# Layer norms of a two-layer encoder: epsilon added on VectorE, and the last token block's statistics taken piece by piece

## The chip, the cores and the metric

The kernel runs on one core of a Trainium2 chip. A core has a matrix engine (TensorE, PE in the rows, with its weight loads as PEld), three engines that work on elements (VectorE as DVE, ScalarE as ACT, GpSimd as POOL), a queue engine that issues most transfers (SyncE, SP), and 16 DMA engines. The metric is the device time of one execution in microseconds, as a median over runs.

## The reference

The reference is an encoder of two layers over 512 tokens of width 1024. Each layer has four phases: a feed-forward half step, a token mixer, an attention into 256 memory tokens, and another feed-forward half step. After each phase stands a post layer norm, so there are eight, each over the 1024 columns of every token:

```python
def layer_norm(x, g, b):
    xf = x.astype(jnp.float32)
    mu = xf.mean(-1, keepdims=True)
    var = jnp.square(xf - mu).mean(-1, keepdims=True)
    return ((xf - mu) * lax.rsqrt(var + LN_EPS) * g.astype(jnp.float32) + b.astype(jnp.float32)).astype(x.dtype)

# each layer:
#   x <- LN(alpha*x + 0.5*SwiGLU_1(x))
#   x <- LN(alpha*x + Mixer_i(x))
#   x <- LN(alpha*x + MemCrossAttn(x, mem))
#   x <- LN(alpha*x + 0.5*SwiGLU_2(x))
```

Everything is in fp32. The mixer of the first layer is a dense attention beside a windowed one, that of the second a neighbourhood attention.

## The kernel before

The eight phases run in the order ffn(0), mixer_ab, memory(0), ffn(1), ffn(2), mixer_c, memory(1), ffn(3). The tokens lie in four blocks of 128, the tiles x_4_85, x_5_86, x_6_87 and x_7_88 (blocks 0 to 3), each 128 x 1024 and resident in SBUF. "The last block" is block 3, x_7_88.

To keep fp32 accuracy, each factor of a product is split into a rounded high part and a rest, and a product is three matmuls (`mm3`: high by high, high by rest, rest by high). The features of x, transposed, lie in xh and xl, one slice of columns per block. Weights are loaded as fp32 (tiles slab and raw), and split by ScalarE (a cast) and VectorE (a subtraction, the TENSOR_TENSOR rows slab<-raw,slab). So VectorE feeds TensorE with weight parts all along, as well as doing its share of the layer norms.

A phase ends in `down` (L538): for each block and each half of 512 columns, six to twelve matmuls into a PSUM bank of tag d or a (each 12 in the mixers and the memory phases, 6 in an FFN, where earlier products have been added to x before), and then one VectorE operation that adds the product to x, x<-d,x or x<-a,x, which also sums what it writes (a DVE_READ_ACCUMULATOR row fetches the sum, into st). There follows `layer_norm` (L505) for the block:

1. nmu<-st, VectorE, one column: minus the mean.
2. slab<-x,nmu,slab, VectorE, 1024 columns: y = (x - mean) * g.
3. junk<-x,nmu, ScalarE: the squares of x - mean, with their sum in var.
4. lny<-var on GpSimd (TENSOR_SCALAR): var / 1024 + epsilon; then lny<-lny,nhalf on GpSimd (TENSOR_TENSOR): that to the power -1/2. Both stand in `rsqrt` (L466).
5. x<-slab,lny,slab, VectorE: y * lny + b. One operation of 1024 columns for blocks 0 and 1, two of 512 for blocks 2 and 3.

After it, in the last phase, each piece goes out by DMA. In the other seven phases `to_features` (L475) makes two rounds of four TensorE transposes (t<-ident,x, 128 x 128 each), one for each half, ScalarE copies each into xh (a cast), and VectorE subtracts for xl (xl<-t,xh). The next phase's products read xh and xl, those of block 3 last of all.

What sets the order: nothing is issued where it stands in the code. All calls are recorded in a graph, and a list scheduler (`plan`, L182, called twice from `emit`, L300) simulates the engines with a table of costs (`cost`, L113) and puts each engine's instructions in an order, which is then fixed; each engine works it off in order, waiting where it has to. The first plan gives each instruction a due time, which is counted back from the order on TensorE; the second plan takes the ready instruction with the earliest due time. Every instruction therefore has line 157 in the profile, and the names of tiles tell what it is. The cost table takes the columns of an instruction from what it writes, except for a reduction:

```python
for d in (out if method != "tensor_reduce" else ins[0]).ap[1:]:
    n *= d[1]
...
if engine == "vector":
    if method == "tensor_scalar" and not wide:
        n = n / 2
    return n / 0.96 + 72 + aside + 60 * scalars + 120 * (method == "scalar_tensor_tensor" and "accum_out" in kw)
```

In ffn the last down product is called from `finish` (L927), for blocks 0 and 1, and then 2 and 3; in the last phase block 2 and block 3 apart.

## Time and profile before

| quantity | value |
|---|---|
| runs, us | 2128.41, 2127.75, 2125.88; median 2127.75 |
| span of the profiled execution | 2123.9 us (no other time of that execution is given) |
| PE busy | 2109.2 us (99%), 12648 matmuls |
| VectorE busy | 1735.8 us (82%), 2500 instructions |
| ScalarE busy | 1161.2 us (55%), 1903 instructions |
| GpSimd busy | 287.4 us (14%), 379 instructions |
| granted TensorE clock | 1.00 for nearly the whole span |
| start of the last matmuls, end of the span | 2111.61 us, 2123.9 us |

Times in rows are microseconds from the span's start. A row of the timeline has start and duration, engine, operation, what is written <- what is read, and how many in a run (x2); a bracket behind it is the engine's idle time before it, and what ended that. Neighbouring operations of a pipelined engine overlap: a row of 0.69 us is often followed 0.61 us after its start. The span lies 3.85 us below the median of the runs.

### The profile page before, as it was taken

How to read it: one execution, taken by the hardware profiler on the slowest of the kernel's cores; microseconds unless marked ns; L12 is line 12 of the kernel's file. 1: busy time of each engine (PE TensorE's matmuls, PEld its weight loads, DVE VectorE, ACT ScalarE, POOL GpSimd, SP SyncE). 2: the span in 40 equal slices, each digit the busy share in tenths (PEclk: the TensorE clock that was granted, in tenths of full speed). 3: DMA queues.
4: the chain of work that ended last, by engine and by line, in shares of the span. 5: the costliest groups of instructions: out<-in, count | busy, mean ns of one | idle time of the engine just before them, and what ended most of it. 6: DMA issues, size and time to landing. Idle time of an engine off the chain costs nothing.

```text
span 2123.9 us, 32745 instructions
## 1 busy us (share of the span) xinstructions
PE 2109.2 (99%) x12648; PEld 1871.0 (88%) x12648; DVE 1735.8 (82%) x2500; ACT 1161.2 (55%) x1903; POOL 287.4 (14%) x379
## 2 busy tenths in 40 slices
PE   9999999999999999999999999999999999999997
PEld 7999988888888899998889999888888888999996
DVE  7789988888748879998879999866577479699997
ACT  5555443698546554545545455457764465444552
POOL 0001015310102000000200000312210021000003
PEclk9999999999999999999999999999999999999999
DMA  6566562004434346564445556356454433456551
GB/s 205 141 168 144 136 191 91 21 18 116 140 125 109 90 117 181 150 158 129 148 100 143 126 139 186 78 147 165 119 165 155 139 93 96 110 149 155 143 149 60
DMA packets 208860, 275.93 MB, mean 130 GB/s; under 512 B 10688, under 2 KB 151616, under 8 KB 208704
## 3 DMA queue, kind: packets, MB, share of 16 engines
q1 hardware_dynamic: 175904, 221.14, 34.0%
q0 software_dynamic: 32512, 52.44, 14.1%
q8 instruction: 100, 1.64, 0.3%
q14 instruction: 56, 0.46, 0.1%
q10 hardware_dynamic: 288, 0.26, 0.0%
HBM read 259.12 MB, written 4.19 MB: 124 GB/s over the span
## 4 chain that ended last, share of the span: by engine, by line
PE 96%; DVE 1%; ACT 1%; DMA 1%; issue 0%; SPq 0%; DVEq 0%; ACTq 0%
PE a L157 59%; PE d L157 23%; PE t L157 15%; DVE slab L157 1%; ACT t L157 1%; DMA slab<-t 1%; DVE x L157 0%; ACT slab L157 0%; SPq L157 0%; DVE t L157 0%; DMA raw<-x_t 0%; ACT xh L157 0%; DVE mn L157 0%; DVE xl L157 0%; DVEq L1662 0%
## 5 line engine op out<-in xcount | busy, mean ns | idle before, releaser
L157 DVE TENSOR_TENSOR slab<-slab,slab 128x1024 fp32r<-128x1024 f32 (+3 forms) x638 | 727.5, 1166 | 69.5 <-ACT slab L157 39.9
L157 ACT CAST slab<-slab 128x1024 fp32r<-128x1024 f32 (+2 forms) x498 | 472.7, 983 | 341.5 <-DVE slab L157 173.2
L157 PE MATMUL a<-slab,slab 128*128 128x256 f32 (+3 forms) x2320 | 567.2, 322 | 0.7 <-DMA slab<-t 0.4
L157 PE MATMUL a<-xh,slab 128*128 128x256 f32 (+2 forms) x2480 | 559.9, 315 | 0.3 <-ACT slab L157 0.3
L157 PE MATMUL d<-slab,slab 128*128 128x512 f32 (+2 forms) x1856 | 447.0, 381 | 0.0
L157 PEld LDWEIGHTS a<-xh,slab 128*128 128x128 f32 x2480 | 416.4, 190 | 33.7 <-ACT slab L157 1.0
L157 PEld LDWEIGHTS a<-slab,slab 128*128 128x128 f32 x2320 | 409.5, 190 | 38.8 <-ACT t L157 1.3
L157 PE MATMUL a<-xl,slab 128*128 128x256 f32 (+1 forms) x1240 | 389.7, 314 | 0.0
L157 PE MATMUL a<-raw,slab 128*128 128x256 f32 x2048 | 388.9, 283 | 0.1
L157 PEld LDWEIGHTS d<-slab,slab 128*128 128x128 f32 x1856 | 329.0, 189 | 55.9 <-issue 0.2
L157 PEld LDWEIGHTS a<-raw,slab 128*128 128x128 f32 x2048 | 327.9, 192 | 5.4 <-ACT slab L157 0.5
L157 PEld LDWEIGHTS a<-xl,slab 128*128 128x128 f32 x1240 | 236.0, 190 | 18.4 <-DVE xl L157 0.4
L157 PE MATMUL t<-slab,slab 128*128 128x512 f32 (+1 forms) x840 | 209.5, 389 | 0.0
L157 DVE TENSOR_TENSOR slab<-raw,slab 128x1024 fp32r<-128x1024 f32 (+2 forms) x140 | 160.2, 1160 | 18.6 <-ACT slab L157 18.4
L157 PEld LDWEIGHTS t<-slab,slab 128*128 128x128 f32 x840 | 149.9, 189 | 26.3
L157 DVE TENSOR_TENSOR slab<-t,slab 128x512 fp32r<-128x512 f32 (+2 forms) x223 | 137.6, 638 | 16.4 <-ACT slab L157 15.9
L157 ACT CAST slab<-t 128x512 fp32r<-128x512 f32 (+2 forms) x223 | 120.9, 566 | 40.7 <-DVE t L157 13.9
L157 ACT CAST slab<-raw 128x1024 fp32r<-128x1024 f32 (+1 forms) x132 | 124.3, 971 | 27.9 <-PE a L157 8.8
L157 DVE SCALAR_TENSOR_TENSOR x<-d,x 128x512 f32<-128x512 f32 x168 | 114.7, 685 | 25.3 <-PE d L157 24.4
L157 ACT COPY t<-a 128x512 f32<-128x512 f32 (+1 forms) x116 | 63.5, 550 | 130.4 <-PE a L157 77.2
L157 POOL DMA_DIRECT2D slab<-ffn_w_down x40 | 47.7, 1193 | 310.3 <-DVE slab L157 276.3
L157 ACT ACTIVATE t<-a 128x512 f32<-128x512 f32 (+3 forms) x65 | 36.3, 559 | 89.0 <-PE a L157 89.0
(126 smaller groups left out, 2167.2 us busy)
## 6 DMA issues: line engine op xcount, KB each, us to landing
slab<-ffn_w_gate SPq DMA_DIRECT2D x80, 512.0 KB
slab<-ffn_w_up SPq DMA_DIRECT2D x80, 512.0 KB
slab<-ffn_w_down SPq DMA_DIRECT2D x80, 512.0 KB
slab<-ffn_w_down POOLq DMA_DIRECT2D x40, 512.0 KB, 5.8
raw<-mem_w_kv SPq DMA_DIRECT2D x16, 1024.0 KB
slab<-t SPq DMA_DIRECT2D x96, 128.0 KB
slab<-ffn_w_gate POOLq DMA_DIRECT2D x16, 512.0 KB, 7.8
slab<-ffn_w_up POOLq DMA_DIRECT2D x16, 512.0 KB, 6.0
```

The source lines that it names most:

```text
L157: op.call = lambda: fn(*args, **kw)
```

## The change

Three things are changed.

- In all eight layer norms, for every block, the step var / 1024 + epsilon moves from GpSimd to VectorE. The power stays on GpSimd.
- For block 3, in all eight, the statistics come from batch-statistics instructions: after each piece of x is added, BN_STATS on VectorE reads that piece and writes six values; after the last, BN_AGGR makes mean and variance of the 18 values (mv). There is then no ScalarE square, no nmu and no accumulated sum for this block, and y = (x - mean) * g is made in two halves.
- For block 3, the second half of the down product, 512 columns in one bank of tag a, becomes two products of 256 columns, one in a bank of tag a and one in a bank of tag d, each with its own addition to x.

```diff
@@ layer_norm
-        nmu = self.small(1, "nmu", 4)
-        nc.vector.tensor_scalar(nmu, st[:, 0:1], st[:, 1:2], -1.0 / D, ALU.add, ALU.mult)
-        var = self.small(1, "var", 4)
...
         y = gb[2][t % 2]
-        nc.vector.scalar_tensor_tensor(out=y, in0=x, scalar=nmu, in1=g, op0=ALU.add, op1=ALU.mult)
-        nc.scalar.activation(self.junk, x, AF.Square, bias=nmu, scale=1.0, accum_out=var)
-        r = self.rsqrt(var, 1, "ln", 1.0 / D, LN_EPS / ALPHA**2)
+        r = self.small(1, "lny", 4)
+        halves = [(0, 512), (512, D)] if t > 1 else [(0, D)]
+        if t == NT - 1:
+            mv = self.small(2, "mv", 2)
+            nc.vector.bn_aggr(out=mv, in_=st)
+            nc.vector.tensor_scalar(r, mv[:, 1:2], LN_EPS / ALPHA**2, None, ALU.add)
+            nc.gpsimd.tensor_tensor(out=r, in0=r, in1=self.nhalf[:, :1], op=ALU.pow)
+            for lo, hi in halves:
+                nc.vector.scalar_tensor_tensor(
+                    out=y[:, lo:hi], in0=x[:, lo:hi], scalar=mv[:, 0:1], in1=g[:, lo:hi], op0=ALU.subtract, op1=ALU.mult
+                )
+        else:
+            nmu = self.small(1, "nmu", 4)
+            nc.vector.tensor_scalar(nmu, st[:, 0:1], st[:, 1:2], -1.0 / D, ALU.add, ALU.mult)
+            var = self.small(1, "var", 4)
+            nc.vector.scalar_tensor_tensor(out=y, in0=x, scalar=nmu, in1=g, op0=ALU.add, op1=ALU.mult)
+            nc.scalar.activation(self.junk, x, AF.Square, bias=nmu, scale=1.0, accum_out=var)
+            nc.vector.tensor_scalar(r, var, 1.0 / D, LN_EPS / ALPHA**2, ALU.mult, ALU.add)
+            nc.gpsimd.tensor_tensor(out=r, in0=r, in1=self.nhalf[:, :1], op=ALU.pow)
         for lo, hi in halves:
             nc.vector.scalar_tensor_tensor(
                 out=x[:, lo:hi], in0=y[:, lo:hi], scalar=r, in1=b[:, lo:hi], op0=ALU.mult, op1=ALU.add
@@ down
         for t in blocks:
-            st = self.small(2, "st", 4) if ln else None
-            for h in range(2):
-                ps = self.ps("da"[h])
+            apart = ln and t == NT - 1
+            st = self.small(18, "bn", 2) if apart else self.small(2, "st", 4) if ln else None
+            cuts = [(0, 512, "d"), (512, 768, "a"), (768, D, "d")] if apart else [(0, 512, "d"), (512, D, "a")]
+            for j, (lo, hi, tag) in enumerate(cuts):
+                ps = self.ps(tag)[:, : hi - lo]
                 for i in range(n):
                     a = [z[:, t * P : (t + 1) * P] for z in acts[i]]
-                    w = [z[:, h * 512 : (h + 1) * 512] for z in wts[i]]
-                    self.mm3(ps, a, w, i == 0, i == n - 1)
-                v = self.x[t][:, h * 512 : (h + 1) * 512]
-                acc = {"accum_out": st[:, h : h + 1]} if ln else {}
+                    self.mm3(ps, a, [z[:, lo:hi] for z in wts[i]], i == 0, i == n - 1)
+                v = self.x[t][:, lo:hi]
+                acc = {"accum_out": st[:, j : j + 1]} if ln and not apart else {}
                 nc.vector.scalar_tensor_tensor(out=v, in0=ps, scalar=coef, in1=v, op0=ALU.mult, op1=ALU.add, **acc)
+                if apart:
+                    nc.vector.bn_stats(out=st[:, 6 * j : 6 * j + 6], in_=v)
```

The cost table prices BN_STATS by the six values it writes, 6 / 0.96 + 72, about 78 ns in the planner, whatever it reads. The scheduler's order changes with the instructions. Three places follow, each as the order of one engine. In the names, x_6_87 and x_7_88 are blocks 2 and 3, d_ and a_ PSUM banks, t_ the banks of transposes, st, nmu, var, lny, bn and mv the small tiles, xh_83 and xl_84 the features, and slab the rest (weights, g, b and y).

First, VectorE in the last phase, from the last addition to x of block 2 to its end. Before:

```order
L157 TENSOR_SCALAR nmu_3848<-st_3845 128x1
L157 SCALAR_TENSOR_TENSOR x_7_88<-d_3851,x_7_88 128x512
L157 SCALAR_TENSOR_TENSOR x_4_85<-slab_3832,lny_3833,slab_3826 128x1024
L157 SCALAR_TENSOR_TENSOR x_5_86<-slab_3839,lny_3840,slab_3826 128x1024
L157 SCALAR_TENSOR_TENSOR x_7_88<-d_3851,x_7_88 128x512
L157 SCALAR_TENSOR_TENSOR x_7_88,st_3852<-d_3853,x_7_88 128x512
L157 SCALAR_TENSOR_TENSOR x_7_88,st_3852<-a_3854,x_7_88 128x512
L157 TENSOR_SCALAR nmu_3855<-st_3852 128x1
L157 SCALAR_TENSOR_TENSOR slab_3832<-x_6_87,nmu_3848,slab_3825 128x1024
L157 SCALAR_TENSOR_TENSOR slab_3839<-x_7_88,nmu_3855,slab_3825 128x1024
L157 SCALAR_TENSOR_TENSOR x_6_87<-slab_3832,lny_3850,slab_3826 128x512 x2
L157 SCALAR_TENSOR_TENSOR x_7_88<-slab_3839,lny_3857,slab_3826 128x512 x2
```

And with the change (the rows just before these are x_5_86 normed, one addition to x_7_88, x_4_85 normed and nmu_3849 for block 2):

```order
L157 SCALAR_TENSOR_TENSOR x_7_88<-d_3851,x_7_88 128x512
L157 SCALAR_TENSOR_TENSOR x_7_88<-d_3853,x_7_88 128x512
L157 SCALAR_TENSOR_TENSOR x_7_88<-a_3854,x_7_88 128x256
L157 SCALAR_TENSOR_TENSOR x_7_88<-d_3855,x_7_88 128x256
L157 BN_STATS bn_3852<-x_7_88 128x6 x3
L157 SCALAR_TENSOR_TENSOR slab_3830<-x_6_87,nmu_3849,slab_3825 128x1024
L157 BN_AGGR mv_3857<-bn_3852 128x2
L157 TENSOR_SCALAR lny_3848<-var_3850 128x1
L157 TENSOR_SCALAR lny_3856<-mv_3857 128x1
L157 SCALAR_TENSOR_TENSOR slab_3837<-x_7_88,mv_3857,slab_3825 128x512 x2
L157 SCALAR_TENSOR_TENSOR x_6_87<-slab_3830,lny_3848,slab_3826 128x512
L157 SCALAR_TENSOR_TENSOR x_7_88<-slab_3837,lny_3856,slab_3826 128x512
```

Behind these follow the second halves of x_6_87 and x_7_88. All three BN_STATS stand behind the last addition, and y of block 2 behind them; the norms of blocks 2 and 3 alternate by halves.

Second, VectorE at the end of the first phase, ffn(0), from the addition to x of block 2 on. Before:

```order
L157 TENSOR_SCALAR nmu_599<-st_596 128x1
L157 SCALAR_TENSOR_TENSOR slab_578<-x_6_87,nmu_599,slab_571 128x1024
L157 SCALAR_TENSOR_TENSOR x_7_88,st_604<-d_605,x_7_88 128x512
L157 TENSOR_SCALAR nmu_607<-st_604 128x1
L157 SCALAR_TENSOR_TENSOR x_6_87<-slab_578,lny_601,slab_572 128x512 x2
L157 TENSOR_TENSOR slab_618<-raw_614,slab_617 128x1024
L157 TENSOR_TENSOR xl_84<-t_602,xh_83 128x4x128
L157 SCALAR_TENSOR_TENSOR slab_587<-x_7_88,nmu_607,slab_571 128x1024
L157 TENSOR_TENSOR xl_84<-t_590,xh_83 128x4x128
L157 SCALAR_TENSOR_TENSOR x_7_88<-slab_587,lny_609,slab_572 128x512 x2
```

With the change, from the second addition to block 3 on (ahead of it stand nmu_600, y of block 2, its epsilon lny_599 and the first addition, x_7_88<-d_605):

```order
L157 SCALAR_TENSOR_TENSOR x_7_88<-a_606,x_7_88 128x256
L157 SCALAR_TENSOR_TENSOR x_6_87<-slab_576,lny_599,slab_572 128x512 x2
L157 SCALAR_TENSOR_TENSOR x_7_88<-d_607,x_7_88 128x256
L157 BN_STATS bn_604<-x_7_88 128x6 x3
L157 BN_AGGR mv_609<-bn_604 128x2
L157 TENSOR_TENSOR xl_84<-t_602,xh_83 128x4x128
L157 TENSOR_SCALAR lny_608<-mv_609 128x1
L157 SCALAR_TENSOR_TENSOR slab_585<-x_7_88,mv_609,slab_571 128x512 x2
L157 SCALAR_TENSOR_TENSOR x_7_88<-slab_585,lny_608,slab_572 128x512
L157 TENSOR_TENSOR xl_84<-t_590,xh_83 128x4x128
L157 TENSOR_TENSOR slab_618<-raw_614,slab_617 128x1024
L157 SCALAR_TENSOR_TENSOR x_7_88<-slab_585,lny_608,slab_572 128x512
```

slab_618, a weight part for the next phase, was ahead of block 3's norm and now stands between its halves; before, the other half of block 3 was added earlier, from bank a_606.

Third, TensorE at the same place, around the transposes of block 3. Before:

```order
L157 MATMUL a_659<-slab_615,xh_83 128x512
L157 MATMUL t_610<-ident_78,x_7_88 128x128 x4
L157 MATMUL a_659<-slab_616,xh_83 128x512
L157 MATMUL t_611<-ident_78,x_7_88 128x128 x4
L157 MATMUL a_659<-slab_615,xl_84 128x512
```

With the change:

```order
L157 MATMUL a_659<-slab_617,xh_83 128x512
L157 MATMUL t_610<-ident_78,x_7_88 128x128 x4
L157 MATMUL a_643<-slab_618,xh_83 128x512
L157 MATMUL a_643<-slab_617,xl_84 128x512
L157 MATMUL a_643<-slab_617,xh_83 128x512
L157 MATMUL t_611<-ident_78,x_7_88 128x128 x4
L157 MATMUL a_643<-slab_618,xh_83 128x512
```

The transposes of the second half stand three matmuls behind those of the first instead of one, and a product that needs slab_618 now stands between them.

More of the change, by code (lines that the diff above doesn't have):

```diff
@@ L509, in layer_norm @@
         x = self.x[t]
-        halves = [(0, 512), (512, D)] if t > 1 else [(0, D)]
-        nmu = self.small(1, "nmu", 4)
-        nc.vector.tensor_scalar(nmu, st[:, 0:1], st[:, 1:2], -1.0 / D, ALU.add, ALU.mult)
-        var = self.small(1, "var", 4)
         if len(gb) < 3:
```

## The prediction

> **What bounds the kernel now.** I read the totals first, then the chain of work that ended last.
>
> ```profile
> span 2123.9 us, 32745 instructions
> PE 2109.2 (99%) x12648; PEld 1871.0 (88%) x12648; DVE 1735.8 (82%) x2500; ACT 1161.2 (55%) x1903; POOL 287.4 (14%) x379
> PE 96%; DVE 1%; ACT 1%; DMA 1%; issue 0%; SPq 0%; DVEq 0%; ACTq 0%
> ```
>
> TensorE sets the time nearly everywhere. Work on other engines costs something only where TensorE has to wait for it: at the seams between phases, where the transposes of block 3 wait for its layer norm, and after the last matmul. So next I read the engines' busy time in four windows: the seam from ffn(0) to the mixer, the 20 us behind it, the seam from ffn(2) to mixer_c, and the end.
>
> ```profile
> core 0: us, PE busy (x) PEld busy (x) DVE busy (x) ACT busy (x) POOL busy (x), PEclk, DMA share, GB/s
> 331.50:350.30 18.80, 18.77 (x97) 15.24 (x96) 17.71 (x29) 6.00 (x12) 6.61 (x8) 1.00 0.15 47
> 350.30:370.00 19.70, 19.70 (x91) 16.30 (x90) 15.14 (x35) 9.09 (x15) 9.31 (x13) 1.00 0.51 170
> 1381.00:1392.30 11.30, 10.09 (x56) 7.80 (x54) 11.09 (x21) 3.71 (x7) 2.63 (x7) 1.00 0.00 0
> 2113.20:2123.90 10.70, 0.00 (x0) 0.00 (x0) 6.29 (x11) 1.24 (x2) 1.93 (x2) 0.68 0.53 178
> ```
>
> At the first seam VectorE is busy for 17.71 of 18.80 us while TensorE still just keeps going; at the other it is busy for 11.09 of 11.30, and TensorE already loses 1.2. VectorE has no spare time there. At the end TensorE does nothing for 10.7 us. The granted clock is full in all windows with matmuls, so it is no term. An edit that gives VectorE more to do at these places is paid for, even if GpSimd and ScalarE are relieved.
>
> **Prices.** The rows of VectorE at the first seam, those of the square on ScalarE, the uses of tile lny on GpSimd (shortest, median and longest in ns), and two groups:
>
> ```profile
> 340.39 0.69 DVE L157 SCALAR_TENSOR_TENSOR x<-d,x 128x512 f32<-128x512 f32 x1
> 341.01 0.08 DVE L157 DVE_READ_ACCUMULATOR x<-d,x 128x1 f32 x1
> 341.13 0.21 DVE L157 TENSOR_SCALAR nmu<-st 128x1 f32<-128x1 f32 x1
> 341.38 1.28 DVE L157 SCALAR_TENSOR_TENSOR slab<-x,nmu,slab 128x1024 f32<-128x1024 f32 x1
> 342.58 0.68 DVE L157 SCALAR_TENSOR_TENSOR x<-d,x 128x512 f32<-128x512 f32 x1
> 344.96 1.22 DVE L157 TENSOR_TENSOR slab<-raw,slab 128x1024 fp32r<-128x1024 f32 x1
> 346.09 0.68 DVE L157 TENSOR_TENSOR xl<-t,xh 128x512 fp32r<-128x512 f32 x1
> 348.49 1.40 DVE L157 SCALAR_TENSOR_TENSOR x<-slab,lny,slab 128x512 f32<-128x512 f32 x2
> 341.43 1.15 ACT L157 ACTIVATE junk<-x,nmu 128x1024 bf16<-128x1024 f32 x1 [4.50 <-issue]
> 342.48 0.19 ACT L157 ACTIVATION_READ_ACCUMULATOR junk<-x,nmu 128x1 f32 x1
> L157 POOL TENSOR_TENSOR lny<-lny,nhalf x32: 550/556/1472, 329.5 to 2117.0; 128x1 f32<-128x1 f32 x32
> L157 POOL TENSOR_SCALAR lny<-var x32: 183/192/1290, 328.6 to 2115.9; 128x1 f32<-128x1 f32 x32
> L157 DVE TENSOR_REDUCE mn<-a 128x1 f32<-128x512 f32 x32 | 20.9, 680 | 0.4 <-PE a L157 0.2
> L157 DVE TENSOR_TENSOR t<-a,t 128x256 f32<-128x256 f32 x26 | 10.7, 419 | 7.9 <-ACT t L157 7.9
> ```
>
> An operation's successor starts about 0.08 us before its end (341.01 against 340.39 + 0.69), so these stand for steps of 0.61 us (512 columns from a bank), 1.20 (1024 with a scalar operand), 1.13 (a weight part), 0.60 (xl), 0.66 (a half norm: 1.40 less 0.08, halved), 0.60 (a reduction of 512) and 0.34 (256 columns). A one-column operation takes 0.12 to 0.25 (341.01 to 341.13, 341.13 to 341.38).
>
> No row shows BN_STATS. It reads 512 or 256 columns, as TENSOR_REDUCE does, so I price the three at 0.60 + 0.34 + 0.34 = 1.28 us for each norm. Bounds: below, 3 x 0.12 = 0.36, if each cost no more than a one-column operation; above, two passes over the columns, 2.56. BN_AGGR reads 18 values: 0.12 to 0.25, like nmu. I take the middle price, since work by the column is what all wide VectorE rows show.
>
> What is removed for block 3 on VectorE is short: two reads of a sum and nmu, some 0.4 us. The square on ScalarE (341.43 to 342.67, 1.2 us) and GpSimd's addition (0.19) go too, but VectorE has other rows to do meanwhile, so that they cost something only where VectorE pauses for them. For the other blocks the addition moves from GpSimd (0.19) to VectorE (0.13), where whatever is queued behind it waits for ScalarE's sum.
>
> **The change on TensorE.** Twelve or six matmuls of 512 become twice as many of 256. The chain gives their step:
>
> ```profile
> 2055.72 2.87 PE a L157 x24
> 2061.34 21.76 PE a L157 x96
> ```
>
> These are runs of 256 columns (2.87 / 24 = 0.1197) and of 512 (21.76 / 96 = 0.2267). So 24 x 0.1197 - 12 x 0.2267 = 0.15 us in each of four phases, half of that in each of the four FFNs: **+0.9 us**, with nothing to cover it. [...]
>
> **The end.**
>
> ```profile
> 2108.44 0.21 DVE L157 TENSOR_SCALAR nmu<-st 128x1 f32<-128x1 f32 x1
> 2109.74 2.47 DVE L157 SCALAR_TENSOR_TENSOR x<-slab,lny,slab 128x1024 f32<-128x1024 f32 x2
> 2112.13 1.49 DVE L157 SCALAR_TENSOR_TENSOR x<-d,x 128x512 f32<-128x512 f32 x2
> 2113.54 0.69 DVE L157 SCALAR_TENSOR_TENSOR x<-a,x 128x512 f32<-128x512 f32 x1
> 2114.27 0.21 DVE L157 TENSOR_SCALAR nmu<-st 128x1 f32<-128x1 f32 x1
> 2114.40 2.47 DVE L157 SCALAR_TENSOR_TENSOR slab<-x,nmu,slab 128x1024 f32<-128x1024 f32 x2
> 2116.79 2.73 DVE L157 SCALAR_TENSOR_TENSOR x<-slab,lny,slab 128x512 f32<-128x512 f32 x4
> 2111.61 1.52 PE L157 MATMUL a<-slab,slab 128*128 128x512 f32 x6
> 2115.93 0.99 POOL L157 TENSOR_SCALAR lny<-var 128x1 f32<-128x1 f32 x1 [3.31 <-ACT junk L157]
> 2117.01 0.94 POOL L157 TENSOR_TENSOR lny<-lny,nhalf 128x1 f32<-128x1 f32 x1
> ```
>
> VectorE runs without a pause from 2109.74 to the end: the last half norm starts at 2116.79 + 3 x 0.66 = 2118.78. The changed order, replayed with these steps from 2108.44: norm of block 1 to 2109.64, addition 2110.25, norm of block 0 2111.45, nmu 2111.58; a wait for TensorE to about 2111.9, since only eleven 256-column matmuls (1.32 us) now stand behind the product awaited; additions of 0.80, 0.60, 0.34 and 0.34 to 2114.0; BN_STATS 1.28 to 2115.3; y of block 2, 1.20, to 2116.5; BN_AGGR and two epsilons, 0.4, to 2116.9; y of block 3 in halves, 1.32, to 2118.2; then four half norms of 0.66, the last from 2120.15. That is late by **+1.35 us**, and so is the last transfer, which waits for it. The pieces do spread the additions, but all the statistics stand behind the last one. (That SyncE now sends block 1 ahead of block 0 costs nothing: both are done some 7 us before the last piece.)
>
> **The first seam.** The transposes it ends with:
>
> ```profile
> 349.56 0.60 PE L157 MATMUL t<-ident,x 128*128 128x128 f32 x4
> 350.23 0.60 PE L157 MATMUL t<-ident,x 128*128 128x128 f32 x4
> ```
>
> Now the second half norm of block 3 starts 8.76 us after block 2's last addition (340.39 to 349.15), and its transposes at 350.23. In the changed order: addition, nmu and y of block 2 to 2.18; a wait for ScalarE's sum (342.67) and epsilon, to 2.51; additions 0.61 and 0.34; block 2's norm 1.33, to 4.79; addition 0.34; BN_STATS 1.28, BN_AGGR 0.25, to 6.7; xl 0.60, epsilon 0.13; y 1.32, to 8.75; the first half 0.66, xl 0.60, then slab_618 1.13; the second half starts at 11.15. Block 2's last product stands some 0.2 us earlier on TensorE, so that half ends at 340.2 + 11.15 + 0.74 = 352.1, and the transposes start at 352.2, 2.0 us later than now. By then TensorE has issued nine 512-column matmuls fewer and six of 256 more than now (9 x 0.2267 - 6 x 0.1197 = 1.3 us still to do), since the products between wait for slab_618 or for block 3. **+3.3 us.** VectorE's spare time behind the seam (15.14 of 19.70) doesn't give this back, for TensorE there is busy throughout.
>
> **The other seams.** Rows of the seam into mixer_c, and of the one behind memory(0):
>
> ```profile
> 1389.15 0.68 DVE L157 TENSOR_TENSOR slab<-raw,slab 128x512 fp32r<-128x512 f32 x1
> 1391.96 0.60 PE L157 MATMUL t<-ident,x 128*128 128x128 f32 x4
> 711.72 1.40 DVE L157 SCALAR_TENSOR_TENSOR x<-slab,lny,slab 128x512 f32<-128x512 f32 x2
> 712.69 0.60 PE L157 MATMUL t<-ident,x 128*128 128x128 f32 x4
> ```
>
> Into mixer_c the same replay ends block 3's second half at 1392.5 instead of 1391.96 (0.6 late) with 1.4 us less issued on TensorE by then (4.0 against 5.4 us of matmuls behind block 3's last product), and the weight part of 1389.15 now stands behind the norm (0.4): **+2.4**. After memory(0) the first half is ready at 711.72 + 0.74 = 712.46 and TensorE takes it at 712.69: 0.2 us of slack. The replay has it ready between 713.2 and 713.9, against a turn at 713.0: +0.45, and the same after memory(1). After mixer_c +0.4. After mixer_ab and ffn(1) some 1 us of slack takes most: +0.5 for both. Together **+2.25**.
>
> **Sum:** 0.9 + 1.35 + 3.3 + 2.4 + 0.45 + 0.45 + 0.4 + 0.5 = 9.75. The span becomes 2123.9 + 9.75 = 2133.65 us; the span lies 3.85 below the median of the runs, so **2137.5 us**.
>
> **The rivals.**
>
> *The seams hide it.* TensorE waits at a seam, but VectorE and ScalarE, whose weight parts don't depend on the norm, run ahead meanwhile, and TensorE then loses less in the phase that follows. Then the split and the end stay, 0.9 + 1.35 = 2.25 us, and of the seams' 7.5 us a quarter at most that isn't won back, 1.9: +2.25 to +4.15, **2130 to 2132**. For it: VectorE's 15.14 of 19.70 us behind the first seam. Against: TensorE is busy throughout those 19.70 us, so there is nothing to win there. A low price of BN_STATS points the same way: at 0.36 in place of 1.28 the end comes to +0.4, the small seams to nothing, the first to 2.4 and that into mixer_c to 1.5, with the split 5.2 in all, 2133.
>
> *BN_STATS takes two passes.* 1.28 us more at seven exposed places (the end and six seams), 9 in all: **2146**. For it: a variance beside a mean is more work than one sum. Against: TENSOR_REDUCE and the additions with a sum run at one column rate.
>
> *GpSimd's power starves.* y of block 3 in halves reads two SBUF tiles without a break while both powers are due. If a power can run only when that is over, block 2's ends 0.55 us behind it, at 2118.75 instead of before 2118.2, and the half norms start as late: 0.55 more, **2138.0**. Against: the power at 2117.01 was lengthened to 0.94 us, but ended at 2117.95 amid back-to-back half norms. [...]
>
> *The chain gets shorter.* Block 3's chain no longer passes through the square (1.2 us) and GpSimd's addition (0.19 to 1.29 us). Where VectorE paused for that chain, its norm comes sooner; this decides if such a pause is longer than the 1.28 us of BN_STATS. Then the seam into mixer_c gives back up to the 1.2 us that TensorE loses there, and the end up to 2.2 (the square, and the addition of 0.99 at 2115.93): 0.9 - 1.2 - 2.2 = -2.5, **2125.2**, and less still if the norms at other seams let TensorE start sooner. Against: VectorE's 11.09 of 11.30 us, and the end's rows, which leave no pause.
>
> **How the numbers follow.** Forecast 0.55, seams hide it 0.22, two passes 0.12, starved power 0.03, shorter chain 0.08. About 0.2% (4.3 us) is what a measurement of this kernel can tell from no change, so slower begins at 2132.0 and faster below 2123.5. The forecast, two passes and starvation are slower, 0.70. The hidden case and three of the eight hundredths of the shorter chain lie between, 0.25; 0.05 is left for faster. The range, 2129.8 to 2143.0, takes in the hidden case from its lower end, the low price of BN_STATS, and a price well on the way to two passes (5.5 of the 9 us); it leaves out two passes in full and the shorter chain. The forecast's own range is 2133 to 2142.
>
> **What would show it.** BN_STATS rows of some 0.68 and 0.42 us on VectorE. At the end, VectorE without a pause from the last additions on, and the last half norm starting 1.3 us later after the last matmul than now. At the first seam, TensorE idle for some 3 us ahead of block 3's second transposes, where it is not idle now; in the seam into mixer_c some 3.6 us lost instead of 1.2 in the window. 256-column matmuls of block 3 stepping by 0.12 us. BN_STATS at about 0.1 us, transposes of block 3 that start as early as now, or a shorter end would each prove its term wrong; a sum under 2130 would prove the replay of the seams wrong altogether.

## The result, and the profile after

The changed kernel takes 2141.14 us (median of 4 runs, 2139.99 to 2142.77) against 2127.59 us for the kernel before; the ratio is 1.0064, with a 95% interval of 1.0050 to 1.0079. That is 13.6 us slower (10.6 to 16.8). The forecast was slower, 2137.5 us in a range of 2129.8 to 2143.0: the direction and the range held, and the sum of 9.75 us was nearly 4 us too small.

The profiled execution has a span of 2141.0 us. It was the slowest of the four (2142.77), and that of the kernel before, at 2123.9, must have been one of its fastest: spans lie 1.7 to 2.2 us below their times wherever both are given, so that about half of the 3.85 us between that span and the median was the chance of one execution. The two profiles differ by 17.1 us, 3.5 more than the medians, and what differs by chance has to be told from what the change did.

The totals of the changed kernel:

```profile
span 2141.0 us, 32872 instructions
PE 2116.7 (99%) x12720; PEld 1877.6 (88%) x12720; DVE 1754.5 (82%) x2556; ACT 1151.9 (54%) x1887; POOL 272.0 (13%) x347
```

VectorE's busy time rises by 18.7 us, while ScalarE (9.3) and GpSimd (15.4) are relieved. The work has moved onto the engine that was full at the seams (17.71 of 18.80 us at the first, 11.09 of 11.30 at the one into mixer_c).

BN_STATS in the view of tile bn, with shortest, median and longest duration in ns:

```profile
L157 DVE BATCH_NORM_STATS2 bn<-x x24: 407/411/686, 344.6 to 2130.6; 128x6 f32<-128x256 f32 x16, 128x6 f32<-128x512 f32 x8
L157 DVE BATCH_NORM_AGGREGATE mv<-bn x8: 227/236/236, 346.0 to 2132.1; 128x2 f32<-128x18 f32 x8
```

It costs what other VectorE operations on as many columns cost: up to 686 ns for 512 and a median of 411 over all 24, most of them of 256, against 680 for the reduction of 512 and 419 for the TENSOR_TENSOR of 256 in the groups before. The end, on VectorE:

```profile
2129.29 0.42 DVE L157 SCALAR_TENSOR_TENSOR x<-d,x 128x256 f32<-128x256 f32 x1
2129.63 1.34 DVE L157 BATCH_NORM_STATS2 bn<-x 128x6 f32<-128x512 f32 x3
2130.89 1.27 DVE L157 SCALAR_TENSOR_TENSOR slab<-x,nmu,slab 128x1024 f32<-128x1024 f32 x1
2132.07 0.23 DVE L157 BATCH_NORM_AGGREGATE mv<-bn 128x2 f32<-128x18 f32 x1
2132.22 0.10 DVE L157 TENSOR_SCALAR lny<-var 128x1 f32<-128x1 f32 x1
2132.34 0.15 DVE L157 TENSOR_SCALAR lny<-mv 128x1 f32<-128x1 f32 x1
2132.41 1.40 DVE L157 SCALAR_TENSOR_TENSOR slab<-x,mv,slab 128x512 f32<-128x512 f32 x2
2133.73 2.73 DVE L157 SCALAR_TENSOR_TENSOR x<-slab,lny,slab 128x512 f32<-128x512 f32 x4
```

From the last addition to the last half norm there is no pause, and the three statistics take 1.26 us (2129.63 to 2130.89). At the first seam, TensorE in the changed kernel:

```profile
345.32 0.73 PE L157 MATMUL a<-slab,xh 128*128 128x512 f32 x2 [0.24 <-ACT xh L157]
346.82 0.50 PE L157 MATMUL a<-slab,xl 128*128 128x512 f32 x1 [0.76 <-DVE lny L157]
348.90 0.63 PE L157 MATMUL t<-ident,x 128*128 128x128 f32 x4 [0.66 <-issue]
350.59 0.50 PE L157 MATMUL a<-slab,xh 128*128 128x512 f32 x1 [1.06 <-DVE slab L157]
351.39 0.60 PE L157 MATMUL t<-ident,x 128*128 128x128 f32 x4
```

The brackets add up to 2.7 us of waiting where there was next to none. The largest but one, 0.76, had no place in the forecast. Its releaser is shown as lny, but the matmul reads xl, whose subtraction had just ended on VectorE, behind the three BN_STATS:

```profile
344.61 1.33 DVE L157 BATCH_NORM_STATS2 bn<-x 128x6 f32<-128x512 f32 x3
346.13 0.63 DVE L157 TENSOR_TENSOR xl<-t,xh 128x512 fp32r<-128x512 f32 x1
```

The wait of 0.66 is for the first half norm of block 3, and the last, 1.06, is for slab_618, as foreseen.

The seam into mixer_c, in windows of 2 us of the changed kernel (columns as in the windows before):

```profile
1392.00:1394.00 2.00, 1.66 (x12) 0.96 (x10) 2.00 (x5) 0.70 (x2) 0.00 (x0) 1.00 0.00 0
1394.00:1396.00 2.00, 0.81 (x2) 0.30 (x2) 2.00 (x5) 0.47 (x1) 0.00 (x0) 1.00 0.00 0
1396.00:1398.00 2.00, 1.70 (x7) 1.14 (x7) 1.97 (x6) 0.00 (x0) 1.19 (x4) 0.81 0.00 0
1398.00:1400.00 2.00, 1.32 (x6) 1.02 (x6) 2.00 (x4) 0.00 (x0) 0.00 (x0) 0.50 0.00 0
1400.00:1402.00 2.00, 2.00 (x8) 1.68 (x7) 1.82 (x4) 1.27 (x3) 0.00 (x0) 0.50 0.00 0
1402.00:1404.00 2.00, 2.00 (x7) 1.64 (x6) 1.26 (x3) 0.52 (x1) 0.00 (x0) 0.50 0.80 234
1404.00:1406.00 2.00, 2.00 (x13) 1.75 (x12) 1.35 (x2) 0.83 (x3) 0.00 (x0) 0.98 0.82 285
```

VectorE is full (2.00 of 2.00) while TensorE waits, and then the granted clock of TensorE falls to 0.50 for 6.8 us: 7 or 8 matmuls in 2 us, where 13 are done at a clock of 0.98 (1404:1406). This is the part of the loss that the forecast had ruled out. VectorE's rows ahead of it show the same order as at the first seam, an xl behind the three BN_STATS, and TensorE waits 1.46 us for it, until 1396.30:

```profile
1394.32 1.34 DVE L157 BATCH_NORM_STATS2 bn<-x 128x6 f32<-128x512 f32 x3
1395.57 0.67 DVE L157 TENSOR_TENSOR xl<-t,xh 128x512 fp32r<-128x512 f32 x1
```

### The profile page after: what moved, and what is told of

The parts are those of the page before. It is cut to its first block, busy times and chain, and to the rows that moved or that the text cites. A ratio compares the mean times of both kernels' runs of the same rounds, so it can differ in the third digit from the quotient of the medians.

```text
span 2141.0 us, 32872 instructions
## 1 busy us (share of the span) xinstructions
PE 2116.7 (99%) x12720; PEld 1877.6 (88%) x12720; DVE 1754.5 (82%) x2556; ACT 1151.9 (54%) x1887; POOL 272.0 (13%) x347
## 5 line engine op out<-in xcount | busy, mean ns | idle before, releaser
L157 PE MATMUL a<-slab,slab 128*128 128x256 f32 (+3 forms) x2320 | 560.0, 319 | 3.0 <-DMA slab<-t 1.8
L157 PE MATMUL d<-slab,slab 128*128 128x512 f32 (+2 forms) x1928 | 458.7, 378 | 0.2 <-DVE x L157 0.2
L157 PEld LDWEIGHTS d<-slab,slab 128*128 128x128 f32 x1928 | 338.8, 189 | 56.1 <-DVE x L157 0.4
L157 ACT CAST slab<-raw 128x1024 fp32r<-128x1024 f32 (+1 forms) x132 | 124.2, 970 | 35.1 <-DMA raw<-mem_w_kv 11.2
L157 DVE SCALAR_TENSOR_TENSOR x<-d,x 128x512 f32<-128x512 f32 (+1 forms) x176 | 118.3, 674 | 24.0 <-PE d L157 23.3
```

Source lines behind the costliest of these rows:

```text
L157: op.call = lambda: fn(*args, **kw)
```

## The experiments

Two views carry the readings. One is the median of runs beside the kernel before. That kernel was run again beside each group of runs, and its median moved between 2126.73 and 2127.59 us; where times of two groups are compared, the ratios are the safer guide. The other is a table of steps: where the first transposes of block 0 stand for each norm, read from the timeline, and the differences from one norm to the next. A step holds the seam of its first norm and the stage behind it. In us:

| step | before | before, again | changed | changed, again | fifth seam as before | first and fifth as before |
|---|---|---|---|---|---|---|
| start to norm 1 | 331.8 | 332.4 | 331.3 | 331.9 | 332.1 | 332.2 |
| norm 1 to 2 | 203.3 | 203.2 | 207.2 | 209.1 | 206.5 | 203.1 |
| norm 2 to 3 | 159.0 | 159.0 | 159.7 | 160.6 | 160.7 | 160.6 |
| norm 3 to 4 | 341.7 | 342.3 | 342.3 | 342.3 | 342.3 | 342.3 |
| norm 4 to 5 | 337.6 | 338.8 | 340.6 | 339.1 | 339.1 | 340.3 |
| norm 5 to 6 | 230.2 | 231.5 | 237.2 | 236.7 | 230.4 | 231.1 |
| norm 6 to 7 | 159.6 | 159.6 | 160.0 | 160.0 | 160.1 | 160.0 |
| norm 7 to last matmul | 349.6 | 349.6 | 350.8 | 350.8 | 350.8 | 351.0 |
| last matmul to end | 11.2 | 11.3 | 12.0 | 12.0 | 12.1 | 12.1 |

**Each kernel twice.** The second profile of the kernel before:

> The kernel before once more, for a second profile. Theory I: two executions of one kernel differ by chance at a few places: the 1024-column split beside GpSimd's additions near 1360 us takes either 2.4 or 3.6 us, and the stages of attention differ by 1 to 2 us; the seams of the norms are alike to 0.1 us. Rival: the places where the changed kernel lost time differ as much between two profiles of the kernel before, so that the seams' losses can't be read from single profiles.

Its one time was 2129.48 us. The steps are alike within 0.13 us, but for four: 0.6 at the start, 0.6 between norms 3 and 4, 1.15 between 4 and 5, and 1.3 between 5 and 6. Theory I holds in the main, and the rival falls: five steps (norm 1 to 2, 2 to 3, and from norm 6 on) can be read from single profiles of this kernel, four others only to about 1 us. What kind of stage a step holds doesn't tell which: of the four, three hold feed-forward stages, and the one with the first mixer is steady. The second profile of the changed kernel:

> The changed kernel once more, for a second profile. If the losses at the norms belong to the change, the steps from norm to norm repeat: 3.9 us by the second norm, 0.6 to 0.7 each in the next two, 0.4 and 1.2 behind the sixth and seventh, 0.9 at the end, each within 0.1. Between the fifth norm and the sixth, 7.0 us in the first profile: if the halved clock there follows from the waits, it is there again, with 5.5 us or more; if it was chance, the clock stays full and 3 us less are lost. The long split near 1365 us takes 2.4 or 3.6 us by chance.

Its time was 2144.08 us. Four of the nine steps repeat within 0.1 us, as was expected of six. Two of those did not: norm 1 to 2 took 5.8 us more than before instead of 3.9, and norm 2 to 3 took 1.6 instead of 0.7. The step from norm 5 to 6 costs 6.5 us again, and the clock is halved there again. At the first seam the granted clock is down too, this time; the windows about the two seams and in mixer_c, in the second profile:

```profile
338.00:360.00 22.00, 19.28 (x86) 15.10 (x85) 18.29 (x36) 6.00 (x11) 3.32 (x5) 0.92 0.28 96
1382.10:1406.00 23.90, 21.23 (x105) 16.93 (x104) 22.28 (x42) 8.11 (x14) 2.29 (x6) 0.86 0.08 22
1406.00:1620.00 214.00, 210.96 (x1217) 183.06 (x1216) 132.76 (x308) 141.95 (x340) 35.62 (x87) 1.00 0.56 154
```

0.92 over 22 us is 1.8 us of full clock lost; in the first profile the same waits (0.24, 0.76, 0.66 and 1.06 us, in both) left the clock at 1.00. So these waits repeat from one execution to the next, and the half clock behind them does not.

**BN_STATS made short, the order kept.**

```diff
-                    nc.vector.bn_stats(out=st[:, 6 * j : 6 * j + 6], in_=v)
+                    nc.vector.bn_stats(out=st[:, 6 * j : 6 * j + 6], in_=v[:, :32])
```

> The changed kernel with each BN_STATS reading only 32 columns of its piece; every engine's order is the same, row by row (the statistics are of a part of the columns only, so the output isn't the layer norm's). Theory A, BN_STATS' columns lie open on VectorE at the seams and at the end: the three cost some 0.4 us in place of 1.26, so the end and the two large seams give back 0.85 each, the five small ones 0.3 to 0.5 each, 4 to 4.5 us in all; and if the wait into mixer_c then no longer halves TensorE's granted clock (0.50 at 1398 to 1404 in the changed kernel's profile), 3 us more: about 2134. Rival B, the new order, the split and the epsilon adds cost the time and BN_STATS is hidden: 2140 to 2142, and the clock dips as before.

It took 2138.13 us (2135.17 to 2140.99), ratio 1.0049 (1.0036 to 1.0061): 3.0 us less than the changed kernel by the medians, and still 10.4 more than the kernel before. The interval overlaps that of the changed kernel, so the size of the gain is uncertain. A row of BN_STATS of 32 columns takes 0.18 us, so the three cost 0.3 to 0.4. Theory A's first figure, 4 to 4.5 without the clock, is nearer than B's, but neither is met: by the medians the columns of BN_STATS are less than a third of the loss. The profile shows which waits they made. The wait for xl at the first seam (0.76) is gone, and the one at the fifth is 0.49 instead of 1.46:

```profile
346.12 0.50 PE L157 MATMUL a<-slab,xl 128*128 128x512 f32 x1
1393.38 0.51 PE L157 MATMUL a<-slab,xl 128*128 128x256 f32 x2 [0.49 <-DVE xl L157]
```

The end is 1.0 us shorter (11.0), near the 0.85 expected. The clock dips at both seams, to 0.93 over each, although the waits are shorter (2.0 and 2.1 us, against 2.7 and 2.5 in the changed kernel).

**Epsilon alone.**

```diff
-        r = self.rsqrt(var, 1, "ln", 1.0 / D, LN_EPS / ALPHA**2)
+        r = self.small(1, "lny", 4)
+        nc.vector.tensor_scalar(r, var, 1.0 / D, LN_EPS / ALPHA**2, ALU.mult, ALU.add)
+        nc.gpsimd.tensor_tensor(out=r, in0=r, in1=self.nhalf[:, :1], op=ALU.pow)
```

> The kernel before with only the epsilon step moved from GpSimd to VectorE, for all blocks; no batch statistics, no split. Theory A: 0.13 us of VectorE work for each block, the chain to the power 0.06 to 0.1 shorter; 0 to +1 us, 2127.5 to 2128.6. Rival B, VectorE's queue now stands behind ScalarE's sum of squares at every norm, and what is behind it is late: +0.4 at eight places and more, 2131 or above.

It took 2132.44 us (11 runs), ratio 1.0019 (1.0010 to 1.0028), 4 to 5 us slower: rival B's figure. The end of this kernel shows how; rows of VectorE, and the power on GpSimd:

```profile
2120.04 2.47 DVE L157 SCALAR_TENSOR_TENSOR slab<-x,nmu,slab 128x1024 f32<-128x1024 f32 x2
2122.43 0.21 DVE L157 TENSOR_SCALAR lny<-var 128x1 f32<-128x1 f32 x2
2123.30 2.74 DVE L157 SCALAR_TENSOR_TENSOR x<-slab,lny,slab 128x512 f32<-128x512 f32 x4 [0.67 <-POOL lny L157]
2122.72 1.06 POOL L157 TENSOR_TENSOR lny<-lny,nhalf 128x1 f32<-128x1 f32 x2 [10.41 <-DVE lny L157]
```

Both epsilons stand behind y of blocks 2 and 3, 2.4 us. Block 2's sum was there by about 2115.7, an estimate: its nmu stands at 2114.07, and in the kernel before the sum is read 1.6 us after the start of nmu (2108.44 to 2110.02). The power on GpSimd starts behind the epsilons, at 2122.72, and VectorE then waits 0.67 us for it. In the kernel before the step ran on GpSimd, at 2110.10 and 2115.93, beside VectorE's norms and y (2109.74 to 2116.87). Here the step costs not its own 0.1 to 0.2 us but its place in VectorE's queue. The end is 1.0 us of the loss, and the step from norm 1 to 2 another 1.0 (204.3); the steps between norms 4 and 6 are 2.1 longer than in the second profile of the kernel before, and that the same order makes these is not shown.

**The split alone** (with accumulated sums and the square kept; one more one-column operation adds the third sum).

```diff
...
-            for h in range(2):
-                ps = self.ps("da"[h])
+            cuts = [(0, 512, "d"), (512, 768, "a"), (768, D, "d")] if ln and t == NT - 1 else [(0, 512, "d"), (512, D, "a")]
+            for j, (lo, hi, tag) in enumerate(cuts):
+                ps = self.ps(tag)[:, : hi - lo]
...
+        if t == NT - 1:
+            nc.vector.scalar_tensor_tensor(out=nmu, in0=st[:, 2:3], scalar=-1.0 / D, in1=nmu, op0=ALU.mult, op1=ALU.add)
```

> The kernel before with only the split of block 3's second half into two products of 256 columns, with accumulated sums, square and GpSimd's epsilon as before (one more one-column operation adds the third sum). Theory A: TensorE's 0.9 us and 0.3 us on VectorE at the end, 2128.5 to 2129.5, no dip of the granted clock. Rival C: 5 us or more above the kernel before.

It took 2132.44 us (11 runs), ratio 1.0020 (1.0011 to 1.0029): 4 to 5 us, near rival C and well over the 0.9 us that the matmul steps explain. By its steps the loss is small at the first seam (0.9), in the last phase (0.9) and at the end (-0.3); most is between norms 5 and 6, 4.1 us over the first profile of the kernel before (2.8 over the second), of which 3.1 (2.1) are waits of TensorE inside mixer_c, behind the seam. What makes TensorE wait there is open.

**No split, the rest of the change kept.**

```diff
-            st = self.small(18, "bn", 2) if apart else self.small(2, "st", 4) if ln else None
-            cuts = [(0, 512, "d"), (512, 768, "a"), (768, D, "d")] if apart else [(0, 512, "d"), (512, D, "a")]
+            st = self.small(12, "bn", 2) if apart else self.small(2, "st", 4) if ln else None
+            cuts = [(0, 512, "d"), (512, D, "a")]
```

> The changed kernel without the split: block 3's second half is one product of 512 columns in a bank of tag a, and BN_STATS reads two pieces of 512. Theory A: TensorE's 0.9 us are saved, BN_STATS costs 1.20 in place of 1.26, and the last piece is 0.3 us longer behind the last product, so 2140 to 2141, with the seams as late as in the changed kernel. Rival C, the split itself does it, by a third bank of tag d and the order that follows: within 1.5 us of the kernel before.

It took 2139.88 us, ratio 1.0057 (1.0044 to 1.0069), within theory A's 2140 to 2141 to 0.1. Rival C falls in company: on top of statistics and epsilon, the split costs 1.3 us by the medians, with intervals that overlap. So the parts don't add up: 4 to 5 each for epsilon and split alone, 12 for the change without the split, 13.6 for all. A reading that fits is that where several parts make the same seam late, the latest counts. The statistics alone, without epsilon and split, were not run.

**Epsilon back on GpSimd, the rest kept.**

```diff
-            nc.vector.tensor_scalar(r, mv[:, 1:2], LN_EPS / ALPHA**2, None, ALU.add)
+            nc.gpsimd.tensor_scalar(r, mv[:, 1:2], LN_EPS / ALPHA**2, None, ALU.add)
...
-            nc.vector.tensor_scalar(r, var, 1.0 / D, LN_EPS / ALPHA**2, ALU.mult, ALU.add)
+            nc.gpsimd.tensor_scalar(r, var, 1.0 / D, LN_EPS / ALPHA**2, ALU.mult, ALU.add)
```

> The changed kernel with epsilon back on GpSimd in all norms (batch statistics and split kept). Theory D, formed after the run with epsilon alone (+5 us) and the one with the split alone (+5 us): the move of epsilon to VectorE puts a wait for ScalarE's sum in front of VectorE's queue and costs some 4 to 5 us in any company: 2136 to 2137. Rival E, the losses aren't additive, because a seam is as late as its latest part, and statistics with split alone make the seams as late: 2139 or more.

It took 2138.14 us (2135.12 to 2142.26), ratio 1.0054 (1.0041 to 1.0067): 3.0 us less than the changed kernel by the medians, 2 by the ratios, between theory D and rival E, with runs 7 us apart. It is unclear which of the two is nearer. In its profile TensorE waits 1.9 us at the first seam and 2.3 at the fifth, and the clock stays full at both.

**The fifth norm's seam as before.**

```diff
-            apart = ln and t == NT - 1
+            apart = ln and t == NT - 1
+            if apart:
+                self.norms = getattr(self, "norms", -1) + 1
+                apart = self.norms != 4
```

(and the same condition in `layer_norm`, with block 3's epsilon on GpSimd there).

> The changed kernel, but block 3 of the fifth norm (the seam into mixer_c) is treated as before the change: accumulated sums, square, epsilon on GpSimd, one second half of 512. Theory F, the halved granted clock at 1398 to 1404 follows TensorE's waits at this seam: without them the clock stays at 1.00 there, and 2.4 us of wait and some 3 us of half clock come back, 5 to 6 in all: 2135 to 2136.5. Rival G, the excess of 6 us between this seam and the next norm is spread over the attention of mixer_c: 2 us or less come back, 2139 or more.

The median was 2138.1 us (2135.35 to 2142.09), ratio 1.0055 (1.0041 to 1.0069): 3.0 us less by the medians and 2 by the ratios, short of theory F's 5 to 6 and near the upper bound of rival G's, 2. The profile speaks more clearly, since its step from norm 5 to 6 falls from 237.2 to 230.4 us, with the clock full in the seam and no more wait in mixer_c than before; the two windows:

```profile
1380.70:1401.00 20.30, 18.61 (x102) 15.03 (x101) 19.20 (x36) 9.46 (x17) 3.46 (x7) 1.00 0.02 3
1401.00:1611.00 210.00, 209.47 (x1206) 181.44 (x1205) 132.96 (x310) 141.61 (x340) 37.44 (x87) 1.00 0.58 159
```

In that execution, one of the two fastest of five, the seam's whole loss is gone, F's reading; over all runs it is not shown that as much comes back. Of the spread between its runs, one part has a sign: the slowest (2142.09) has a mean clock of 0.996, the others 0.998, and the first seam is still as late as in the changed kernel.

**The first and the fifth seam as before** (`self.norms not in (0, 4)` in the same places).

> The changed kernel, but block 3 of the first and of the fifth norm (the seams into the two mixers after an FFN) is treated as before the change. Theory K, these two seams with the clock dips that follow them carry most of the loss: by the landmarks of the profiles 3.9 and 7.0 us of it, so some 2130 to 2132, the granted clock full in every window ahead of the end, and a spread between runs no wider than before's 4 us. Rival L, the seams move on to the next place (the planner's new order elsewhere costs as much): 2134 or more.

It took 2134.36 us (2132.51 to 2137.8), ratio 1.0036 (1.0024 to 1.0049), 6.8 us less than the changed kernel, just over rival L's bound and not K's 2130 to 2132. K's figure was made with 10.9 us from one profile of each kernel, of spans that lie 17.1 us apart; the two seams are worth 6.8 of the 13.6 us by medians, some 6 by the ratios. The mean clock was 0.998 in every run and full in every window ahead of the last matmul, as K had it, but the spread was 5.3 us. What L says holds in part: the step from norm 2 to 3, 160.6 us, is as long as in the longer of the changed kernel's two profiles, and 7 us remain against the kernel before.

**The last phase alone** (the changed functions for the eighth norm, those of before for the others).

```diff
-        if t == NT - 1:
+        if t == NT - 1 and last:
...
-            nc.vector.tensor_scalar(r, var, 1.0 / D, LN_EPS / ALPHA**2, ALU.mult, ALU.add)
+            (nc.vector if last else nc.gpsimd).tensor_scalar(r, var, 1.0 / D, LN_EPS / ALPHA**2, ALU.mult, ALU.add)
...
-            apart = ln and t == NT - 1
+            apart = ln and t == NT - 1 and ln["last"]
```

> The kernel before with the whole change in the last phase alone (epsilon on VectorE, batch statistics and split for the eighth norm). Theory A: the end is 0.9 to 1.35 us later and TensorE pays 0.08: +0.9 to +1.5 over the kernel before, which a measurement can hardly tell from nothing. Rival M, the shorter chain helps where nothing else waits: -1 to -2.5.

It took 2128.86 us against 2127.15 (11 and 21 runs), ratio 1.0009 (1.0000 to 1.0018): 1.7 us, a little over theory A's; rival M falls. In the profile the step from norm 7 to the last matmul is 0.7 us longer, and from there to the end it takes 12.5 us instead of 11.2.

**The planner told what BN_STATS reads.**

```diff
-        for d in (out if method != "tensor_reduce" else ins[0]).ap[1:]:
+        for d in (out if method not in ("tensor_reduce", "bn_stats") else ins[0]).ap[1:]:
```

> The changed kernel with the planner told what BN_STATS reads: its price from 512 or 256 columns in place of six values. Instructions are the same, the order differs. Theory A: VectorE's work at the seams is what it is, and an honest price moves it by 0 to 2 us: 2139 to 2141. Rival H, the wrong price makes the bad order, and the honest one wins back most of the seams: 2132 to 2136.

It took 2141.32 us, ratio 1.0069 (1.0056 to 1.0081): theory A (nothing won, 0.3 over its range), rival H falls. The wrong price is not the cause.

**A control: another order of the same instructions.**

```diff
-            return n / 0.96 + 72 + aside + 60 * scalars + 120 * (method == "scalar_tensor_tensor" and "accum_out" in kw)
+            return n / 0.96 + 75 + aside + 60 * scalars + 120 * (method == "scalar_tensor_tensor" and "accum_out" in kw)
```

> A control: the kernel before, with the same instructions, in which only the planner's fixed price of a VectorE instruction is 75 ns in place of 72; TensorE's order differs in 587 lines of its listing, about as much as with epsilon alone (586). Theory A, what costs time is the work and the waits that the change adds: within 2 us of the kernel before. Rival J, any new order of this plan costs a few us, and epsilon alone and the split alone showed that: +3 to +6.

It took 2127.95 us against 2127.15, ratio 1.0005 (0.9997 to 1.0014). Rival J falls for this order at least: another order of the same instructions, with as many lines different as epsilon alone, costs 0.8 us, which can't be told from nothing. It is one other order; that the change's own order costs nothing by itself doesn't follow.

## Why the prediction was right, and where its sum was too small

The table sets each term of the forecast, with its share of the split, against the steps of the two profiles of the changed kernel over the first of the kernel before:

| step | forecast | measured, both profiles |
|---|---|---|
| start to norm 1 | 0.1 | -0.5, 0.1 |
| norm 1 to 2 (first seam) | 3.45 | 3.9, 5.8 |
| norm 2 to 3 | 0.4 | 0.7, 1.6 |
| norm 3 to 4 | 0.5 | 0.6, 0.6 |
| norm 4 to 5 | 0.3 | 2.9, 1.4 |
| norm 5 to 6 (into mixer_c) | 2.55 | 7.0, 6.5 |
| norm 6 to 7 | 0.55 | 0.4, 0.4 |
| norm 7 to last matmul | 0.5 | 1.2, 1.2 |
| the end | 1.35 | 0.9, 0.8 |

The second profile of the kernel before would make the step from norm 4 to 5 1.2 us, that from norm 5 to 6 1.3 us, and the first and that from norm 3 to 4 0.6 us less.

**Bounds and price.** VectorE was the engine to look at, and BN_STATS costs by the column (0.18 us for 32, a median of 0.41 over rows mostly of 256, up to 0.69 for 512): 1.26 us for three, forecast 1.28. Two passes fall. That the seams hide it falls with the waits at both. The starved power does not show at the end: both powers run on GpSimd from 2132.47 to 2134.22, beside y of block 3 (2132.41 to 2133.81), and VectorE has no pause there. The shorter chain falls too, since neither the seam into mixer_c nor the end gave anything back. The split's step held on TensorE (6 matmuls of 256 columns in 0.71 us, 0.12 each, forecast 0.1197):

```profile
1389.36 0.88 PE L157 MATMUL a<-slab,slab 128*128 128x256 f32 x6
1390.07 0.88 PE L157 MATMUL d<-slab,slab 128*128 128x256 f32 x6
```

**Luck in the range.** The range held, but its upper part had been left for a dearer BN_STATS. BN_STATS cost what was forecast, and what filled that room was the clock and waits without a term.

**The first seam.** The replay was good: block 3's second half norm starts 10.8 us after block 2's last addition (350.45 less 339.65), forecast 11.15, before 8.76. The 3.45 us of the forecast are the 3.9 of the first profile; of the 1.9 more of the second, 1.7 to 1.8 are clock.

**The step that failed: the seam into mixer_c, with the sentence that the granted clock is full and so is no term.** That was read from the kernel before, where it is 1.00 at this seam. With the change it falls to 0.50 there, behind waits that the change makes; in the run with this seam as before it stays at 1.00. In the changed kernel the seam and mixer_c:

```profile
1381.00:1405.00 24.00, 21.49 (x106) 17.23 (x105) 21.83 (x43) 8.48 (x15) 2.29 (x6) 0.86 0.11 36
1405.00:1618.18 213.18, 210.36 (x1208) 181.88 (x1207) 132.50 (x308) 141.67 (x339) 36.20 (x87) 1.00 0.56 153
```

And in the kernel before, first and second profile:

```profile
1373.40:1393.20 19.80, 18.59 (x101) 14.98 (x100) 18.88 (x34) 8.39 (x15) 3.38 (x9) 1.00 0.00 1
1393.20:1603.56 210.36, 209.87 (x1211) 182.14 (x1210) 133.32 (x311) 142.11 (x341) 38.50 (x88) 1.00 0.58 159
```

```profile
1395.50:1607.20 211.70, 210.19 (x1211) 182.00 (x1210) 133.41 (x311) 142.35 (x341) 37.94 (x88) 1.00 0.58 158
```

TensorE waits 2.5 us at the seam instead of 1.2. The clock is halved for 6.8 us, and in 6.1 of them TensorE is busy, which costs some 3.1 us. And TensorE waits 2.8 us within mixer_c instead of 0.5 or 1.5. Together that is 5.7 to 6.7 us more, of a step that is 5.7 to 7.0 longer. Of the 2.4 us that were foreseen, all as waits at the seam, 1.3 came; the clock, which had no term, took more than the whole. The waits within mixer_c (3.0 in the second profile) had no term either. The run with the fifth seam as before has 0.5 there, but the run with short BN_STATS, whose seam is late, has 1.0, and the split alone 3.6: what makes them is open.

**Epsilon had no term of its own** beyond 0.13 us a block and one wait at the first seam. Alone it costs 4 to 5 us; at the end, its place in VectorE's queue behind wide operations shows as 1.0 us of them. In the whole change, taking it back wins 3.0 us by the medians and 2 by the ratios, with an interval that can't settle it. The forecast had named the queue, and did not price it.

**The end** was late by 0.8 to 0.9 us in place of 1.35. The last half norm starts 6.75 us behind the start of the last matmul (2133.73 + 3 x 0.66 = 2135.7, less 2128.97), 6.0 before. The replay had VectorE late for its last additions; in fact its last addition starts at 2129.29, as soon as TensorE's last product is there, and VectorE was done with them 0.5 us sooner than replayed. From there on the rows follow the replay within 0.1 us.

**Norm 4 to 5** is chance in good part, shown next.

## What to carry to other kernels

Ask which engine is full at the seam, not which is busiest on average. VectorE is busy for 82% of the span, but was for 17.71 of 18.80 us and 11.09 of 11.30 at two seams; the change that relieves ScalarE by 9.3 us and GpSimd by 15.4 at its expense is, with the split, 13.6 us slower. A one-column operation of 0.1 to 0.2 us that moved into VectorE's queue cost its place in line: alone it cost 4 to 5 us, 1.0 of them at the end, behind 2.4 us of y. Ask what stands ahead of it, and who waits. And the clock of 1.00 in the kernel before did not hold under the waits that the change makes: at seams with 2.0 to 3.6 us of waits on TensorE, stretches of 3.4 or 6.8 us at half clock followed, by an estimate from these lengths up to 1.7 or 3.4 us of loss, in some executions and not in others. It belongs in the range.

## What the runs showed of the hardware that was not expected

**The clock fell without a long gap.** The longest single wait ahead of the fall at 1397 us in the changed kernel, on TensorE, took 1.46 us:

```profile
1396.30 0.51 PE L157 MATMUL a<-slab,xl 128*128 128x256 f32 x2 [1.46 <-DVE xl L157]
```

Others there are of 0.2 to 0.5 us. TensorE was busy for 4.2 of 6 us (1392 to 1398), and had half the clock for 6.8 us from 1397.26. The second profile of the changed kernel shows a stretch of half that length at the first seam:

```profile
348.00:351.41 3.41, 1.69 (x9) 0.99 (x8) 3.41 (x6) 0.59 (x1) 0.51 (x1) 1.00 0.00 0
351.41:354.82 3.41, 3.41 (x11) 2.72 (x11) 3.41 (x5) 0.59 (x1) 0.00 (x0) 0.50 0.66 205
354.82:358.23 3.41, 3.41 (x17) 2.81 (x16) 1.36 (x3) 0.79 (x2) 0.10 (x1) 1.00 1.01 372
```

Up to the last matmul, every stretch at half clock in the profiles of these runs lasted 3.4 or 6.8 us, to the 0.1 us that windows of 4 us resolve. The two falls of this profile, at 351.4 and 1399.3, are 1047.9 us apart, and so are, to 0.1 us, the two of the run with short BN_STATS; what sets that distance is not shown.

How long TensorE waits at a seam doesn't settle whether the clock falls. It stayed at 1.00 at the first seam with 2.7 us of waits in the first profile of the changed kernel and in the run with the fifth seam as before, and with 2.4 in the run in which the planner is told what BN_STATS reads. It fell there with the same 2.7 in the second profile of the changed kernel, and with 2.0 in the run with short BN_STATS. The control with another order shows a dip at the fifth seam (0.82 and 0.75 in the 8 us from 1388) with waits of 1.1 us there, where the kernel before has 1.2 and a clock of 1.00. What decides it is not shown.

**Beside GpSimd's additions a VectorE operation took one of two longer times.** Near 1360 us GpSimd adds six pieces of 512 columns to x while VectorE splits a weight. In the kernel before, and in the changed one with its next TensorE row:

```profile
1359.67 2.38 DVE L157 TENSOR_TENSOR slab<-slab,slab 128x1024 fp32r<-128x1024 f32 x1
1357.18 9.00 POOL L157 TENSOR_TENSOR x<-x,slab 128x512 f32<-128x512 f32 x6
```

```profile
1365.38 3.64 DVE L157 TENSOR_TENSOR slab<-slab,slab 128x1024 fp32r<-128x1024 f32 x1
1362.88 5.05 POOL L157 TENSOR_TENSOR x<-x,slab 128x512 f32<-128x512 f32 x4
1369.70 3.00 POOL L157 TENSOR_TENSOR x<-x,slab 128x512 f32<-128x512 f32 x2 [1.77 <-DVE x L157]
1369.77 3.00 PE L157 MATMUL t<-slab,slab 128*128 128x512 f32 x12 [0.95 <-DVE x L157]
```

A split of 1024 columns takes 1.22 us at 1344.96 in the kernel before, while GpSimd is idle, and 2.4 or 3.6 beside these additions; with 3.6, in the changed kernel, GpSimd stops after four pieces, and TensorE waits 0.95 us for a bank that VectorE empties late. It is not the program: the kernel before has 2.38 in one profile and 3.64 in the other, and the changed kernel 3.64 and 2.39. Of the 14 profiles eight have 3.64 and six 2.38 or 2.39. What decides between the two is not shown. The step from norm 4 to 5 follows it, 337.6 against 338.8 us in the kernel before, 340.6 against 339.1 in the changed one. So it is worth 1.2 to 1.5 us from one execution to the next, by these steps.
